# Two blocks on one NeuronCore: both parts of x as 512 moving columns in retention and the first feed-forward

## The chip, the cores and the metric

The kernel runs on one core of a Trainium2 chip. The metric is the device time of one execution in microseconds; below, the median of three runs stands beside the one execution that was taken with the profiler. All times of rows are in microseconds from the start of the profiled span.

## The reference, cut to what matters

Two transformer blocks of depth 2 run one after the other on 256 tokens of width 1024, all in fp32. The first block has a retention mixer, a SwiGLU feed-forward of width 2816, a stick-breaking attention and a mixture of 8 experts; the second block has a hybrid mixer and a convolution feed-forward, twice. The change touches only the first two stages:

```python
def retention_mixer(x, w_in, w_out):
    proj = x @ w_in
    q, k, v, g = split(proj)               # q, k: 4 heads x 256; v, g: 2048 wide
    q, k = rotary(q), rotary(k * 256 ** -0.5)
    ...                                    # scores, state, group norm -> o
    return (silu(g) * o) @ w_out

def swiglu(x, w_in, w_out):
    gate, up = split(x @ w_in, 2)          # 2816 each
    return (silu(gate) * up) @ w_out
```

## The kernel before, in words

**Units.** All weights are cut into units of 128 partitions x 2048 fp32 values (1 MB), which stream through a ring of 13 buffers (`Stream`, from line 33). SyncE's queue loads a raw unit (line 68). ScalarE makes its high part by a copy that rounds to fp32r (`wh`, line 83), VectorE the low part as the difference (`wl`, line 94). `W.advance()`, called behind each unit, splits the next unit for which there is room; at most five split pairs stand at a time (`PAIRS`), so in the steady state each call makes one `wh` and one `wl`, for a unit some five ahead of the one in use, and then issues the next load. The activations x are split in the same way, into `xh` and `xl`, which are two tiles with tags of their own.

**The product of a unit.** `projA` (lines 205 to 217) makes 256 output features for 256 tokens, features on the partitions. For each of two column halves c and each of eight k there are three matmuls of 256 moving columns, all into the same 256 sums: high weights by `xh`, high weights by `xl`, low weights by `xh` (`mm3`, line 200). That is 48 matmuls and 48 weight loads a unit. The result lies in PSUM in a tile with the tag "P"; there are four of these, of one bank each. The other tag, "A", has two tiles of two banks each; the output projections and the transpositions at the end of a stage use it.

**Order.** The order on every engine is that of the program text: the kernel switches the planner off (`manual_schedule`), so that an instruction waits behind all that stand before it on its engine, even if its own inputs are ready. In all three loops `W.advance()` stands at the end of the body, so the two weight splits of a unit stand ahead of the next unit's work on ScalarE and VectorE.

**The three loops.** (1) Query and key, 8 units: `projA`; `rotary` (lines 350 to 358) forms x cos and x sin on VectorE out of PSUM (tiles `t1` and `t2`, tag "wk" with two buffers), and GpSimd makes from both the subtraction and the addition into `qk`. (2) Gate, 8 units: `projA`, silu on ScalarE (line 441), multiplication with the normalised attention `onT` on VectorE (442), high part `yh` on ScalarE (194), low part `yl` on VectorE (195). (3) Feed-forward, 22 units: the first four come with tokens on the partitions and are transposed, the other 18 through `projA`; then silu of the gate half (456), multiplication with the other half (457), `yh`, `yl`.

**Behind loops 2 and 3** stands the output projection (`proj_out`, line 239): it takes two "A" tiles, one for each half of the tokens, and for each weight unit runs 12 matmuls of 512 columns into the first and then 12 into the second.

Of the kernel before, what the change touches and what calls it, by code (L numbers as in the profile page):

```python
# [10 lines left out]
F32 = mybir.dt.float32  # L11
F32R = mybir.dt.float32r
# [3 lines left out]
AF = mybir.ActivationFunctionType  # L16
OP = mybir.AluOpType
PSUM = bass.MemoryType.PSUM

S, D = 256, 1024  # L20
KC = D // 128
# [5 lines left out]
FT = 22  # L27
E = 8
SL = 7
UNIT = 2048  # L30


class Stream:
# [6 lines left out]
    def __init__(self, nc, pool, pairs, count, units):  # L40
        self.nc, self.units = nc, units
        self.pairs = pairs
        self.free = [(pool, "b%d" % i, len(units)) for i in range(count)]
        self.n_load = self.n_h = self.n_l = self.n_get = self.n_done = 0
        self.rt, self.ht, self.held = {}, {}, {}
# [80 lines left out]
def tok(t):  # L126
    return slice(t * 128, t * 128 + 128)
# [6 lines left out]
class Net:  # L134
# [51 lines left out]
        nc.vector.memset(self.eps_rms, RMS_EPS)  # L186

    def new_xT(self):
        xh = self.xT.tile([128, KC, S], F32R, tag="xh", name="xh")
        xl = self.xT.tile([128, KC, S], F32R, tag="xl", name="xl")  # L190
        return xh, xl

    def split(self, h, l, src, eng=None):
        self.nc.scalar.activation(h, src, AF.Copy)  # L194
# [10 lines left out]
    def projA(self, between=None, apart=False):  # L205

        h, l = self.get8()
        ps = [self.psP([128, S]) for _ in range(2)] if apart else self.psP([128, 2, S])
        for c in range(2):
            if c and between:  # L210
                between(ps)
            s = tok(c)
            self.mm3(ps[c] if apart else ps[:, c, :], [p for k in range(KC) for p in (
                (h[:, k, s], self.xh[:, k, :]), (h[:, k, s], self.xl[:, k, :]), (l[:, k, s], self.xh[:, k, :]))])
        self.W.done()
        return ps

    def tokB(self, ps, w, t):
        h, l = w
# [67 lines left out]
            self.W.done()  # L287
            yield ps[i]

    def features(self, first, n, pool):  # L290

        nc, last = self.nc, None

        def copied(ps):
            x = pool.tile([128, 2, 256], F32, tag="fl", name="fl", bufs=2)
            nc.scalar.activation(x, ps, AF.Copy)
            return x

        def flip(x):
            pt = self.psP([128, 2, S])  # L300
            for c in range(2):
                for t in range(2):
                    nc.tensor.transpose(pt[:, c, tok(t)], x[:, t, tok(c)], self.ident)
            return pt

        k = 0
        for ps in first:
            x = copied(ps)
            if last is not None:
                yield flip(last)  # L310
            last = x
            k += 1
        ps = self.projA()
        yield flip(last)
        yield ps
        for _ in range(n - k - 1):
            yield self.projA()

    def rstd(self, var, eps, scale, n=1, tag="rs"):
        sd = self.small(n, tag + "_sd")  # L320
# [5 lines left out]
    def start(self):  # L326
        nc, a = self.nc, self.a
        self.xh, self.xl = self.new_xT()
        W = self.W
        (xr, sx), (t, sw) = W.take(0, "xr", F32), W.take(0, "raw", F32)  # L330
        (h, sh), (l, sl) = W.take(0, "wh"), W.take(0, "wl")
        fh, fl = (x.rearrange("p k s -> p (k s)") for x in (self.xh, self.xl))
        for p in range(4):
            s = half(p)
            nc.sync.dma_start(xr[:, s], a["xT"][:, s])
            nc.sync.dma_start(t[:, s], W.units[0][:, s])
        for p in range(4):
            s = half(p)
            self.split(fh[:, s], fl[:, s], xr[:, s])
            self.split(h[:, s], l[:, s], t[:, s])  # L340
        W.ht[0] = (h, l)
        W.held[0] = [sh, sl]
        W.free += [sx, sw]
        W.n_load = W.n_h = W.n_l = 1
        W.fill()
        W.advance()
        self.x = self.xt.tile([128, 2, D], F32, name="x")
        nc.sync.dma_start(self.x, a["x"])

    def rotary(self, ps, out, cos, sin, scale, pool):  # L350
        nc = self.nc
        t1 = pool.tile([128, 2, S], F32, tag="wk", name="t1", bufs=2)
        t2 = pool.tile([128, 2, S], F32, tag="wk", name="t2", bufs=2)
        for t, cs in ((t1, cos), (t2, sin)):
            nc.vector.scalar_tensor_tensor(t, ps, scale, cs[:, None, :].to_broadcast([128, 2, S]),
                                           op0=OP.mult, op1=OP.mult)
        nc.gpsimd.tensor_tensor(out[:, 0, :], t1[:, 0, :], t2[:, 1, :], op=OP.subtract)
        nc.gpsimd.tensor_tensor(out[:, 1, :], t2[:, 0, :], t1[:, 1, :], op=OP.add)

    def retention(self):  # L360
        nc, tc, a = self.nc, self.tc, self.a
        W = self.W
        with tc.tile_pool(name="r1", bufs=1) as p, tc.tile_pool(name="r2", bufs=2) as w:
# [20 lines left out]
            def pv(h, t):  # L384
                ps = self.psP([128, 512])
                vs = half(h)
                if t == 0:
                    nc.tensor.matmul(ps, lhsT=sc[:, h, :128], rhs=v[:, 0, vs], start=True, stop=True)
                else:
                    nc.tensor.matmul(ps, lhsT=sc[:, h, 128:256], rhs=v[:, 0, vs], start=True, stop=False)  # L390
                    nc.tensor.matmul(ps, lhsT=sc[:, h, 256:], rhs=v[:, 1, vs], start=False, stop=True)
                st = self.sm.tile([128, 6], F32, tag="st1", name="st1")
                nc.vector.bn_stats(st, ps)
                mv = self.small(2, "mv")
                nc.vector.bn_aggr(mv, st)
                r = self.rstd(mv[:, 1:2], self.eps_ln, 1.0)
                on[h, t] = w.tile([128, 512], F32, tag="wk", name="on")
                nc.vector.tensor_scalar(on[h, t], ps, mv[:, 0:1], r, op0=OP.subtract, op1=OP.mult)

            def tr(h, t):  # L400
                o = on.pop((h, t))
                ps = self.psP([128, 4, 128])
                for j in range(4):
                    nc.tensor.transpose(ps[:, j, :], o[:, tok(j)], self.ident)
                nc.scalar.activation(onT[:, 4 * h:4 * h + 4, tok(t)], ps, AF.Copy)

            for i in range(2):
                for h in range(RH):
                    ps = self.projA()
                    self.rotary(ps, qk[:, i, h], cs[:, 0, :], cs[:, 1, :], 1.0, w)  # L410
                    W.advance()
            nc.scalar.preload_act_table_set("sqrt_and_others")
            todo = []
# [17 lines left out]
            yh = p.tile([128, 16, S], F32R, tag="b0", name="yh")  # L431
            yl = p.tile([128, 16, S], F32R, tag="b1", name="yl")
            for j in range(8):
                ps = self.projA(lambda ps: (tr(2, 1), pv(3, 1)) if j == 0 else None)
                if j < 2:
                    tr(3, j)
                if j == 0:
                    nc.scalar.preload_act_table_set("silu_and_others")
                    joint = LayerNorm(self, p, w, 0, "ds")
                sg = w.tile([128, 2, S], F32, tag="wk", name="sg")  # L440
                nc.scalar.activation(sg, ps, AF.Silu)
                nc.vector.tensor_tensor(sg, sg, onT[:, 2 * j:2 * j + 2, :], op=OP.mult)
                self.split(yh[:, 2 * j:2 * j + 2, :], yl[:, 2 * j:2 * j + 2, :], sg)
                W.advance()
# [3 lines left out]
    def ffn(self, joint0):  # L448
        nc, tc, W = self.nc, self.tc, self.W
        with tc.tile_pool(name="f1", bufs=1) as p, tc.tile_pool(name="f2", bufs=2) as w:  # L450
            joint = LayerNorm(self, p, w, 1)
            yh = p.tile([128, FT, S], F32R, name="yh")
            yl = p.tile([128, FT, S], F32R, name="yl")
            for j, ps in enumerate(self.features(self.head(joint0, "silu"), FT, w)):
                sg = w.tile([128, S], F32, tag="sg", name="sg")
                nc.scalar.activation(sg, ps[:, 0, :], AF.Silu)
                nc.vector.tensor_tensor(sg, sg, ps[:, 1, :], op=OP.mult)
                self.split(yh[:, j, :], yl[:, j, :], sg)
                W.advance()
            self.proj_out(yh, yl, FT // 2, joint)  # L460
            return joint
# [140 lines left out]
    def moe(self, joint0):  # L602
        nc, tc, a, W = self.nc, self.tc, self.a, self.W
        with self.span:
# [51 lines left out]
            low_part(0)  # L656
            logits(1)
            high_part(1)
            W.widen([(self.xT, x, self.moe_i + 70) for x in ("xh", "xl")])
            W.pairs = 3  # L660
            W.fill()
            route(1)
# [610 lines left out]
class Joint:  # L1273
# [17 lines left out]
    def trans(self, t):  # L1291
        n, nc = self.n, self.nc
        if t == 0:
            n.xh, n.xl = n.new_xT()
        src = self.src[t]
        for f in range(2):
            q = n.psA()[:, 0, :].rearrange("p (b c) -> p b c", b=4) if t else n.psP([128, 4, 128])
            for j in range(4):
                nc.tensor.transpose(q[:, j, :], src[:, tok(4 * f + j)], n.ident)
            k = slice(4 * f, 4 * f + 4)  # L1300
            n.split(n.xh[:, k, tok(t)], n.xl[:, k, tok(t)], q)
# [258 lines left out]
```

## Time and profile before

| | |
|---|---|
| median of three runs | 2269.43 us (2269.21 to 2270.16) |
| profiled execution | 2271.13 us, span 2269.3 us, mean granted clock 0.992 |
| TensorE busy | 2209.9 us, 97% |
| VectorE busy | 1705.9 us, 75% |
| ScalarE busy | 1374.1 us, 61% |
| GpSimd busy | 63.4 us, 3% |
| DMA | 562.07 MB, mean 248 GB/s |

Busy time is the time with at least one instruction in work. Matmuls are pipelined: the duration shown of one is from its start to its modelled end, while the next one starts much earlier, so the pace is read from start to start. A row `x2` merges two instructions.

### The profile page before, as it was taken

What the parts mean: (1) busy time and instruction counts of PE and PEld (TensorE: products, weight loads), DVE (VectorE), ACT (ScalarE), POOL (GpSimd) and SP (SyncE); (2) the same over time, 40 slices, a digit from 0 to 9 for tenths busy, and PEclk for the clock granted to TensorE, in tenths of its full rate; (3) what the DMA queues carried; (4) which work ended last, traced back from release to release, by engine and by line L of the source; (5) the groups of instructions that cost most, each with busy time, mean ns of one, the idle gap of its engine ahead of it and who ended that gap; (6) DMA issues with size and microseconds to landing.
All of it is one profiled execution on the core that took longest, in us unless ns stands there. A gap on an engine that the chain in (4) does not pass through costs nothing. (4 is left out here: it accounts for less than half of the span.)

```text
span 2269.3 us, 31847 instructions
## 1 busy us (share of the span) xinstructions
PE 2209.9 (97%) x13077; PEld 1922.5 (85%) x13077; DVE 1705.9 (75%) x1671; ACT 1374.1 (61%) x1380; POOL 63.4 (3%) x78
## 2 busy tenths in 40 slices
PE   8999999998999999999999999997999999999998
PEld 8998998987888888878887888886889998888996
DVE  6566554647889888888888888887876975776972
ACT  4353543664777777777776777775556654555752
POOL 4100000010000000000000000000000000000000
PEclk9999999999999999999999999998999999999999
DMA  8444555537988899989998999995234554434551
GB/s 305 163 170 173 200 186 184 174 129 279 397 328 311 303 386 366 352 309 376 355 351 301 345 377 366 353 345 185 94 131 169 205 186 167 151 130 143 204 192 68
DMA packets 80074, 562.07 MB, mean 248 GB/s; under 512 B 9072, under 2 KB 9136, under 8 KB 13488
## 3 DMA queue, kind: packets, MB, share of 16 engines
q1 hardware_dynamic: 76464, 547.39, 65.7%
q0 software_dynamic: 3456, 12.55, 1.7%
q8 instruction: 105, 1.72, 0.3%
q14 instruction: 49, 0.40, 0.0%
HBM read 558.86 MB, written 1.05 MB: 247 GB/s over the span
## 5 line engine op out<-in xcount | busy, mean ns | idle before, releaser
L94 DVE TENSOR_TENSOR wl<-raw,wh 128x2048 fp32r<-128x2048 f32 x518 | 1185.3, 2291 | 318.8 <-ACT wh L83 316.7
L83 ACT ACTIVATE wh<-raw 128x2048 fp32r<-128x2048 f32 x518 | 991.2, 1915 | 393.7 <-PE pp L754 198.7
L200 PE MATMUL pp<-xh,wh 128*128 128x256 f32 x1360 | 389.0, 286 | 7.5 <-ACT wh L194 7.4
L200 PE MATMUL pp<-xh,wl 128*128 128x256 f32 x1360 | 385.6, 283 | 0.1
L200 PE MATMUL pp<-xl,wh 128*128 128x256 f32 x1360 | 384.3, 283 | 0.0
L200 PEld LDWEIGHTS pp<-xh,wh 128*128 128x128 f32 x1360 | 257.0, 189 | 9.3 <-ACT wh L194 8.1
L200 PEld LDWEIGHTS pp<-xl,wh 128*128 128x128 f32 x1360 | 258.8, 190 | 0.5 <-issue 0.5
L200 PEld LDWEIGHTS pp<-xh,wl 128*128 128x128 f32 x1360 | 257.7, 189 | 1.2 <-DVE wl L195 0.9
L200 PE MATMUL pp<-wh,xh 128*128 128x256 f32 x720 | 206.8, 287 | 5.2 <-DVE mix L1139 5.2
L200 PE MATMUL pp<-wh,xl 128*128 128x256 f32 x720 | 203.1, 282 | 0.0
L200 PE MATMUL pp<-wl,xh 128*128 128x256 f32 x720 | 202.6, 281 | 0.0
L754 PE MATMUL pp<-wh,xgh 128*128 128x512 f32 x448 | 179.5, 401 | 3.8 <-DVEq L831 3.8
L754 PE MATMUL pp<-wh,xh 128*128 128x512 f32 x448 | 179.4, 400 | 0.0
L754 PE MATMUL pp<-wl,xgh 128*128 128x512 f32 x448 | 177.2, 396 | 1.5 <-DVE wl L94 1.5
L754 PE MATMUL pp<-wl,xh 128*128 128x512 f32 x448 | 177.7, 397 | 0.7 <-DVE wl L94 0.7
L754 PE MATMUL pp<-wh,xl 128*128 128x512 f32 x448 | 177.6, 396 | 0.0
L754 PE MATMUL pp<-wh,xgl 128*128 128x512 f32 x448 | 177.0, 395 | 0.0
L200 PEld LDWEIGHTS pp<-wh,xh 128*128 128x128 f32 x720 | 136.6, 190 | 7.9 <-issue 6.1
L764 PE MATMUL pa<-wh,hh 128*128 128x512 f32 x448 | 142.0, 398 | 0.7 <-ACT hh L194 0.7
L764 PE MATMUL pa<-wh,hl 128*128 128x512 f32 x448 | 141.4, 397 | 0.0
L764 PE MATMUL pa<-wl,hh 128*128 128x512 f32 x448 | 141.3, 397 | 0.0
L200 PEld LDWEIGHTS pp<-wl,xh 128*128 128x128 f32 x720 | 136.6, 190 | 0.9 <-issue 0.7
(335 smaller groups left out, 3054.4 us busy)
## 6 DMA issues: line engine op xcount, KB each, us to landing
raw<-in_moe_w_in SPq DMA_DIRECT2D x224, 1024.0 KB, 5.4
raw<-in_moe_w_out SPq DMA_DIRECT2D x112, 1024.0 KB, 5.5
raw<-in_w_up SPq DMA_DIRECT2D x44, 1024.0 KB, 4.8
raw<-in_w_in SPq DMA_DIRECT2D x28, 1024.0 KB, 4.8
raw<-in_ret_w_in SPq DMA_DIRECT2D x23, 1024.0 KB, 5.2
raw<-in_ffn_w_in SPq DMA_DIRECT2D x22, 1024.0 KB, 4.8
raw<-in_w_down SPq DMA_DIRECT2D x22, 1024.0 KB, 4.8
raw<-in_ffn_w_out SPq DMA_DIRECT2D x11, 1024.0 KB, 4.8
```

The source lines that it names most:

```text
L83: self.nc.scalar.activation(h, self.rt[i][0], AF.Copy)
L94: self.nc.vector.tensor_tensor(l, r, h.bitcast(F32), op=OP.subtract)
L200: self.nc.tensor.matmul(out, lhsT=w, rhs=x, start=(i == 0), stop=(i == n - 1))
L754: nc.tensor.matmul(q, lhsT=x[:, k, :], rhs=ww[:, kk, :], start=(k == 0 and i == 0), stop=(k == KC - 1 and i == 2))
L764: nc.tensor.matmul(A[0][f], lhsT=x[:, k, :], rhs=ww[:, kk, half(f)], start=(s == 0 and k == 0 and i == 0), stop=(s == SL - 1 and k == 3 an ...
```

## The change

`xh` and `xl` become two halves of one tile (`xx`). A new `projW` takes the place of `projA` in 7 of the 8 query/key units, in the gate units j = 2 to 7 and in the last 17 units of the feed-forward. Per c and k it runs one matmul of 512 moving columns, `xh` and `xl` side by side, over the high weights, and one of 256 columns, `xh` over the low weights, into the first 256 sums: 32 matmuls a unit. Its result lies in an "A" tile, one bank for each c. ScalarE copies the sums of `xl` to SBUF, and VectorE adds those of `xh`; what follows works on this sum in SBUF, in place. In `rotary` the sine product comes first and the cosine product overwrites the sum; both are plain multiplications. In the mixture of experts, the two halves of the x tile that are lent to the ring for a while come out of one tile.

```diff
     def new_xT(self):
-        xh = self.xT.tile([128, KC, S], F32R, tag="xh", name="xh")
-        xl = self.xT.tile([128, KC, S], F32R, tag="xl", name="xl")
-        return xh, xl
+        self.xx = x = self.xT.tile([128, 2, KC, S], F32R, tag="x", name="xx")
+        return x[:, 0], x[:, 1]
...
+    def projW(self, pool, tag):
+        h, l = self.get8()
+        A = self.psA()
+        x = pool.tile([128, 2, S], F32, tag=tag, name="sum", bufs=2)
+        for c in range(2):
+            s, o = tok(c), A[:, c, :].rearrange("p (j s) -> p j s", j=2)
+            for k in range(KC):
+                self.nc.tensor.matmul(o, lhsT=h[:, k, s], rhs=self.xp[:, :, k, :], start=(k == 0),
+                                      stop=(k == KC - 1))
+                self.nc.tensor.matmul(o[:, 0, :], lhsT=l[:, k, s], rhs=self.xh[:, k, :], start=False,
+                                      stop=(k == KC - 1), skip_group_check=True)
+        self.W.done()
+        self.nc.scalar.activation(x, A[:, :, S:], AF.Copy)
+        self.nc.vector.tensor_tensor(x, A[:, :, :S], x, op=OP.add)
+        return x
...
-            yield self.projA()
+            yield self.projW(pool, "fl") if wide else self.projA()
...
-    def rotary(self, ps, out, cos, sin, scale, pool):
+    def rotary(self, ps, out, cos, sin, pool, own):
         nc = self.nc
-        t1 = pool.tile([128, 2, S], F32, tag="wk", name="t1", bufs=2)
+        t1 = pool.tile([128, 2, S], F32, tag="wk", name="t1", bufs=2) if own else ps
         t2 = pool.tile([128, 2, S], F32, tag="wk", name="t2", bufs=2)
-        for t, cs in ((t1, cos), (t2, sin)):
-            nc.vector.scalar_tensor_tensor(t, ps, scale, cs[:, None, :].to_broadcast([128, 2, S]),
-                                           op0=OP.mult, op1=OP.mult)
+        for t, cs in ((t2, sin), (t1, cos)):
+            nc.vector.tensor_tensor(t, ps, cs[:, None, :].to_broadcast([128, 2, S]), op=OP.mult)
...
-                    ps = self.projA()
-                    self.rotary(ps, qk[:, i, h], cs[:, 0, :], cs[:, 1, :], 1.0, w)
+                    first = i == h == 0
+                    ps = self.projA() if first else self.projW(w, "wk")
+                    self.rotary(ps, qk[:, i, h], cs[:, 0, :], cs[:, 1, :], w, first)
                     W.advance()
...
-                sg = w.tile([128, 2, S], F32, tag="wk", name="sg")
+                if j < 2:
+                    sg = w.tile([128, 2, S], F32, tag="wk", name="sg")
+                else:
+                    sg = ps = self.projW(w, "wk")
                 nc.scalar.activation(sg, ps, AF.Silu)
...
-            W.widen([(self.xT, x, self.moe_i + 70) for x in ("xh", "xl")])
+            lent = self.xT.tile([128, 2, UNIT], F32, tag="x", name="lent")
+            W.widen([(Lent(lent[:, i, :]), None, self.moe_i + 70) for i in range(2)])
```

## Rows read from the trace of the kernel before

**Rows 1.** Page, part 1: busy time, share, instructions.
```profile
PE 2209.9 (97%) x13077; PEld 1922.5 (85%) x13077; DVE 1705.9 (75%) x1671; ACT 1374.1 (61%) x1380; POOL 63.4 (3%) x78
```

**Rows 2.** Windows, three stretches: length, busy (instructions) by engine, granted clock, DMA.
```profile
20.00:55.00 35.00, 35.00 (x294) 35.00 (x293) 27.04 (x24) 16.52 (x9) 18.87 (x11) 1.00 0.84 310
...
270.00:300.00 30.00, 30.00 (x252) 30.00 (x251) 18.05 (x17) 13.71 (x17) 0.00 (x0) 1.00 0.58 206
...
1210.00:1211.00 1.00, 1.00 (x4) 0.81 (x3) 1.00 (x1) 0.00 (x0) 0.00 (x0) 0.50 0.08 33
```

**Rows 3.** Timeline of TensorE, output projection: start, duration, instruction.
```profile
170.13 0.63 PE L239 MATMUL pa<-wh,yh 128*128 128x512 f32 x2
...
172.93 0.63 PE L239 MATMUL pa<-wh,yh 128*128 128x512 f32 x2
```

**Rows 4.** Timelines of VectorE and ScalarE, gate units; in brackets idle time and releaser.
```profile
132.12 0.69 DVE L442 TENSOR_TENSOR sg<-sg,onT 128x512 f32<-128x512 f32 x1 [1.75 <-ACT sg L441]
...
137.53 0.68 DVE L442 TENSOR_TENSOR sg<-sg,onT 128x512 f32<-128x512 f32 x1
...
142.93 0.68 DVE L442 TENSOR_TENSOR sg<-sg,onT 128x512 f32<-128x512 f32 x1
...
131.49 0.60 ACT L441 ACTIVATE sg<-pp 128x512 f32<-128x512 f32 x1
...
138.25 0.63 ACT L194 ACTIVATE yh<-sg 128x512 fp32r<-128x512 f32 x1 [1.39 <-DVE sg L442]
...
141.53 0.60 ACT L441 ACTIVATE sg<-pp 128x512 f32<-128x512 f32 x1 [0.84 <-PE pp L200]
```

**Rows 5.** Timelines of VectorE, ScalarE and TensorE, feed-forward and its output projection.
```profile
267.73 0.41 DVE L457 TENSOR_TENSOR sg<-sg,pp 128x256 f32<-128x256 f32 x1
...
272.64 0.42 DVE L457 TENSOR_TENSOR sg<-sg,pp 128x256 f32<-128x256 f32 x1
...
287.87 0.42 DVE L457 TENSOR_TENSOR sg<-sg,pp 128x256 f32<-128x256 f32 x1 [0.40 <-ACT sg L456]
...
257.44 0.37 ACT L456 ACTIVATE sg<-pp 128x256 f32<-128x256 f32 x1
...
287.45 0.38 ACT L456 ACTIVATE sg<-pp 128x256 f32<-128x256 f32 x1 [2.31 <-PE pp L200]
...
347.58 0.63 PE L239 MATMUL pa<-wh,yh 128*128 128x512 f32 x2
```

**Rows 6.** Timelines of VectorE, GpSimd and ScalarE, query/key units.
```profile
37.47 1.29 DVE L355 SCALAR_TENSOR_TENSOR t<-pp,cs 128x512 f32<-128x512 f32 x2 [1.32 <-POOL qk L358]
38.68 2.28 DVE L94 TENSOR_TENSOR wl<-raw,wh 128x2048 fp32r<-128x2048 f32 x1
42.28 1.29 DVE L355 SCALAR_TENSOR_TENSOR t<-pp,cs 128x512 f32<-128x512 f32 x2 [1.32 <-POOL qk L358]
...
29.83 2.80 POOL L358 TENSOR_TENSOR qk<-t,t 128x256 f32<-128x256 f32 x1
...
38.84 2.71 POOL L357 TENSOR_TENSOR qk<-t,t 128x256 f32<-128x256 f32 x1 [1.40 <-DVE t L355]
...
59.59 1.92 ACT L83 ACTIVATE wh<-raw 128x2048 fp32r<-128x2048 f32 x1 [3.84 <-PE pp L200]
```

**Rows 7.** Timelines of ScalarE and VectorE: a copy out of PSUM, and a dependent pair.
```profile
118.22 0.60 ACT L418 ACTIVATE v<-pp 128x512 f32<-128x512 f32 x1 [2.42 <-PE pp L200]
...
217.90 0.68 DVE L1335 SCALAR_TENSOR_TENSOR z<-x,pa 128x512 f32<-128x512 f32 x1
218.62 0.69 DVE L1336 BATCH_NORM_STATS2 st<-z 128x6 f32<-128x512 f32 x1
```

**Rows 8.** Timeline of TensorE in the mixture of experts, behind a long idle time.
```profile
1207.94 0.47 PE L754 MATMUL pp<-wh,xgh 128*128 128x512 f32 x1 [3.84 <-DVEq L831]
...
1208.72 0.57 PE L754 MATMUL pp<-wh,xgh 128*128 128x512 f32 x1
...
1212.08 0.44 PE L754 MATMUL pp<-wh,xgl 128*128 128x512 f32 x1
```

More of the change, by code (lines that the diff above doesn't have):

```diff
@@ L30, with __init__, tile @@
 UNIT = 2048
+class Lent:
+    def __init__(self, ap):
+        self.ap = ap
+    def tile(self, shape, dt, tag, name):
+        return self.ap if dt == F32 else self.ap.bitcast(dt)
 class Stream:
@@ L288, in head, with features @@
             yield ps[i]
-    def features(self, first, n, pool):
+    def features(self, first, n, pool, wide=False):
         nc, last = self.nc, None
@@ L328, in start @@
         self.xh, self.xl = self.new_xT()
+        self.xp = self.xx
         W = self.W
@@ L433, in retention @@
             for j in range(8):
-                ps = self.projA(lambda ps: (tr(2, 1), pv(3, 1)) if j == 0 else None)
                 if j < 2:
+                    ps = self.projA(lambda ps: (tr(2, 1), pv(3, 1)) if j == 0 else None)
                     tr(3, j)
@@ L453, in ffn @@
             yl = p.tile([128, FT, S], F32R, name="yl")
-            for j, ps in enumerate(self.features(self.head(joint0, "silu"), FT, w)):
+            for j, ps in enumerate(self.features(self.head(joint0, "silu"), FT, w, True)):
                 sg = w.tile([128, S], F32, tag="sg", name="sg")
@@ L1294, in trans @@
             n.xh, n.xl = n.new_xT()
+            n.xp = n.xx
         src = self.src[t]
```

## Prediction, written before the changed kernel ran

> **What bounds the kernel now.** I read the busy shares first: TensorE has work 97% of the span, so a microsecond taken from it or put on it counts in full, unless another engine holds it up [rows 1]. Second, the windows give its pace in the stage that is changed: 294 matmuls of 256 columns in 35.0 us, 119 ns each, at granted clock 1.00 [rows 2]. The timeline gives the pace of 512 columns: twelve matmuls from 170.13 to 172.93, 233 ns each [rows 3]. So the price goes almost by columns: two of 256 cost 238 ns, one of 512 costs 233. Third, because the change gives ScalarE and VectorE more to do per unit, I read their timelines in the three loops that it touches. Those engines take instructions in the order written: the multiplication of unit 2 starts at 142.93, the moment the weight split before it lets VectorE go, though its silu was done at 142.13 [rows 4]. What matters is therefore not their busy share, but how long one turn of their dependent chain is against the 5.71 us (48 x 119 ns) of a unit on TensorE.
>
> **Direct part: matmuls.** 30 units change (7 of the query/key units, 6 gate units, 17 of the feed-forward). Each goes from 48 matmuls of 256 columns (48 x 119 = 5.71 us) to 16 of 512 and 16 of 256 (16 x (233 + 119) = 5.63 us): 0.08 us a unit, 2.4 us in all, where TensorE sets the pace. No row shows a 512-column operand made of two pieces of 256; bounds: two separate matmuls, 238 ns, no gain; or the full 2.4 GHz, some 210 ns by the half clock of [rows 2, 8] (420 ns, halved 210), some 0.4 us a unit. I take 233, the nearest row. The Trainium skill, "TensorE: Matmul & The Clock Gate", section "Back-to-back issue gap", has about 131 ns for a sustained matmul of 512 columns; by that a unit would take 16 x (131 + 119) = 4.0 us and 30 units would give back 51 us; the rows have 233, so I keep them. None of this enters the sum below, since in all three loops the end is set by ScalarE and VectorE.
>
> **What is added.** Per unit one ScalarE copy out of PSUM (128x512: 0.60 us) and one VectorE addition that waits for it (0.69, as the multiplication of the same size) [rows 4, 7]. The old product went into one of four PSUM buffers "P"; the new one uses "A", of which there are two. So unit k+2 can't start before the addition of unit k is done; and behind the gate units and the feed-forward the output projection takes the same two buffers, its first token half that of the last unit but one, its second half that of the last unit.
>
> **Gate units.** One turn before: multiplication, high part of y, weight split on ScalarE, weight split on VectorE, next multiplication: 142.93 - 137.53 = 5.40 us, below 5.71, so it catches up [rows 4]. The changed turn starts with the addition: to the silu that needs it 0.72 (as from multiplication to high part, 137.53 to 138.25), silu to multiplication 0.63 (131.49 to 132.12), then the old 5.40: 6.75 us against a unit of 5.63. The lag grows 1.1 us a unit. The first changed unit (j=2) adds at 142.93, where its multiplication starts now; j=7 adds at 142.93 + 5 x 6.75 = 176.68 and ends at 177.37. Two buffers just cover the units themselves (j=5's addition ends at 163.87, when j=7 may start at about 164.1, four units of 5.65 behind the 141.53 at which j=2's product is ready). But the output projection's second half now starts at 172.93 [rows 3], and after the change at 177.42, 0.05 behind the last addition: **+4.5 us**.
>
> **Feed-forward.** One turn now: 272.64 - 267.73 = 4.91 [rows 5]. Added: addition to silu 0.72, silu to multiplication 0.42 (287.45 to 287.87): 6.05 us against 5.63. The first changed unit (j=5) has its copy where its silu stands now, 257.44, since ScalarE is behind there; addition 0.63 later, at 258.07. The 21st adds at 258.07 + 16 x 6.05 = 354.87, ends 355.56. On the way TensorE waits some 0.4 us before each unit; the second half of the output projection starts at 355.61 and not at 347.58 [rows 5]: **+8.0 us**.
>
> **Query/key units.** Here the sum lies in a "wk" buffer, of which there are two, the other holding the sine product; GpSimd reads both, so the next copy waits for GpSimd. One turn: copy 0.60 + 0.03, addition and the gap before an instruction that reads its result 0.72 (217.90 to 218.62, [rows 7]), sine product 0.61, cosine product 0.69, 0.08 to GpSimd, its two subtractions 3.41 (38.84 to 42.25; the first takes 2.71 as VectorE's weight split runs beside it), 0.03: 6.17 us [rows 6]. Now that turn is 42.28 - 37.47 = 4.81, below a unit, and four buffers cover its late start. The first rotary work ends on GpSimd at 32.63 [rows 6]; the second unit's copy then starts at 32.66, its addition ends at 33.98. Unit k+2 starts 0.05 behind addition k: the eighth starts at 33.98 + 4 x 6.17 + 0.05 = 58.71 and ends 5.63 + 0.16 later at 64.5. It ends at 59.57 now, where the ScalarE split that it releases starts (59.59): **+4.9 us**. The split blocked behind the waiting copy is of a unit four ahead, which hides it; the value units behind use "P" and are not held.
>
> **Clock.** The second halves above find TensorE idle 3.95 us (gate units: the first half ends its issue at 173.47) and about 3.2 us (feed-forward). Behind an idle of 3.84 us the granted clock was 0.50, which is 1.2 GHz, and eight matmuls of 512 columns, from 1208.72 to 1212.08, took 3.36 us and not 1.86: 1.5 us lost [rows 2, 8]. I put 1.5 on the gate units and half of it, 0.7, on the feed-forward (bounds 0 and 1.5 each). The first wait in the query/key units, about 3.5 us, is paid inside the GpSimd turn, which is longer than a unit, so a slow unit there is hidden.
>
> **Neighbours at nothing.** One tile for both parts of x, and the lent tile in the mixture of experts, have the same readers and last uses; they cost nothing if each half keeps its own waits; a false wait there would cost about one weight split, 2.28 us [rows 6], at each place. The weights' transfers start later where VectorE frees their buffers later, but they are split four to five units ahead of their use, some 20 us, which covers that.
>
> **Sum.** Profiled execution 2271.13 (span 2269.3, 1.8 around it). 4.9 + 4.5 + 8.0 + 2.2 = 19.6: span 2288.9, execution 2290.7. The three runs' median, 2269.43, is 1.7 under the profiled one; so 2289.0.
>
> **Rivals.**
> (a) *Not slower: the chains don't hold TensorE.* If the addition ran in the free time of VectorE (it is busy 18.05 of 30 us in the feed-forward now [rows 2], 3.4 us a unit, and would be 4.1 of 5.63), the turns stay under a unit and the direct 2.4 us remain: 2267. It decides from a turn of 5.63 us downward. For it: the busy sums. Against: the start at 142.93, behind the split. 8%. By the 131 ns of the Trainium skill's page (section as above) the same rival would end at 2218; against the rows' 233 ns it gets 1 of these 8.
> (b) *Part of the stalls.* The silu and products out of SBUF are quicker than out of PSUM, or GpSimd's start ahead of the split shortens its turn. At 0.4 us less a turn, the feed-forward loses 16 x 0.4 = 6.4 of its 8.0, the gates 2.0 of 4.5, query/key 1.6 of 4.9, and the clock term goes: 2277. 17%.
> (c) *Only the ends count worse*: both idle times lower the clock in full, and false waits on the joint tile add a split at two places: 2295. 7%.
> (d) *The change doesn't do what it says*: two-piece operands run as two: no different here, 2289, as the chains set the end; it has its chance in the forecast's.
>
> **How the numbers follow.** Forecast 67%, with 2283 to 2294 its own range (0.2 us a turn on 16 + 5 + 4 turns is 5 us; the clock 2). Range: down to (b) with a little less, up to (c): 2273 to 2295. A measurement of this kernel tells 0.2% (4.5 us) from no change. Faster: 4% (half of (a), if the 512 columns are near the lower bound of 210 ns). Same: 9% (the other half of (a), and 5 of (b) at its lowest). Slower: 87%, the rest.
>
> **What would show it.** Right: additions 6.0 to 6.1 us apart in the feed-forward and 6.7 apart in the gates; TensorE's idle time before the "pa" matmuls put down to the addition, with some 4 and 3 us at the output projections; query/key units over 6 us apart. Wrong: matmuls of the changed units without gaps and the output projection starting with the last unit; or 512-column matmuls well under 230 ns with the stage shorter than now.

## The result and the profile after

| | before | after |
|---|---|---|
| median of five runs | 2269.28 us (2269.20 to 2270.16) | 2292.37 us (2291.55 to 2293.51) |
| profiled execution, span | 2271.13, 2269.3 us | 2291.55, 2289.5 us |
| TensorE busy, matmuls | 2209.9 us, 13077 | 2213.1 us, 12597 |
| VectorE, ScalarE busy | 1705.9, 1374.1 us | 1725.8, 1389.9 us |

After over before is 1.0099 (95% interval 1.0087 to 1.0110): 23 us slower, against a forecast of 2289.0. There are 480 matmuls fewer (30 x 16), and ScalarE and VectorE have 30 instructions more each, as meant. The time lies in waits. These are the waits of TensorE's weight loads from 20 to 400 us in the changed kernel (us in total, times, longest):

```profile
PEld pa L235 <- DVE sum L241: 14.1, 19, 3.6
PEld pa L265 <- DVE sum L241: 9.4, 4, 4.1
```

L235 is the wide matmul of a unit, L265 the output projection, L241 the new addition. The two rows are not the loss itself: by the same list for matmuls, TensorE stood idle for 16.0 us before them.

```profile
PE pa L235 <- DVE sum L241: 8.1, 19, 3.3
PE pa L265 <- DVE sum L241: 7.9, 4, 3.7
```

The next rows are TensorE's matmuls that waited, in the same kernel: the first wait of the query/key units, the two halves of the retention's output projection, one of the repeated waits of the feed-forward, and the second half of its output projection.

```profile
33.52 0.80 PE L235 MATMUL pa<-xx,wh 128*128 128x512 f32 x1 [3.29 <-DVE sum L241]
...
175.63 0.74 PE L265 MATMUL pa<-wh,yh 128*128 128x512 f32 x2 [0.91 <-DVE sum L241]
182.41 0.74 PE L265 MATMUL pa<-wh,yh 128*128 128x512 f32 x2 [3.70 <-DVE sum L241]
...
306.56 0.50 PE L235 MATMUL pa<-xx,wh 128*128 128x512 f32 x1 [0.22 <-DVE sum L241]
...
367.48 1.18 PE L265 MATMUL pa<-wh,yh 128*128 128x512 f32 x2 [3.02 <-DVE sum L241]
```

The second halves began at 172.93 [rows 3] and 347.58 [rows 5] before. VectorE in the same kernel shows the turns: gate units first, then feed-forward.

```profile
147.74 0.68 DVE L241 TENSOR_TENSOR sum<-pa,sum 128x512 f32<-128x512 f32 x1
...
154.53 0.68 DVE L241 TENSOR_TENSOR sum<-pa,sum 128x512 f32<-128x512 f32 x1
...
181.67 0.68 DVE L241 TENSOR_TENSOR sum<-pa,sum 128x512 f32<-128x512 f32 x1
...
269.26 0.69 DVE L241 TENSOR_TENSOR sum<-pa,sum 128x512 f32<-128x512 f32 x1
...
275.36 0.68 DVE L241 TENSOR_TENSOR sum<-pa,sum 128x512 f32<-128x512 f32 x1
...
366.74 0.68 DVE L241 TENSOR_TENSOR sum<-pa,sum 128x512 f32<-128x512 f32 x1
```

From 147.74 to 181.67 are five turns, 6.79 us each; from 269.26 to 366.74 sixteen, 6.09 us each. Each addition starts without idle time, and all but the one at 269.26 right behind a weight split, though the ScalarE copy was done before. For the one at 154.53 the copy and the split are:

```profile
152.19 0.57 ACT L240 ACTIVATE sum<-pa 128x512 f32<-128x512 f32 x1
...
152.32 2.29 DVE L104 TENSOR_TENSOR wl<-raw,wh 128x2048 fp32r<-128x2048 f32 x1 [1.11 <-ACT wh L93]
```

In the query/key units the copy waits for GpSimd (ScalarE, 6.30 us from copy to copy):

```profile
38.43 0.60 ACT L240 ACTIVATE sum<-pa 128x512 f32<-128x512 f32 x1 [3.89 <-POOL qk L384]
...
44.73 0.60 ACT L240 ACTIVATE sum<-pa 128x512 f32<-128x512 f32 x1 [3.90 <-POOL qk L384]
```

Three kinds of marks cut the difference into terms: the first multiplication of the gate units (132.12 [rows 4], then 136.93), the second halves above, and the last norm statistics behind each stage (VectorE, before and then after, with the first gate multiplication after):

```profile
220.66 0.21 DVE L1315 BATCH_NORM_AGGREGATE mv<-st 128x2 f32<-128x12 f32 x1
...
412.12 0.21 DVE L1315 BATCH_NORM_AGGREGATE mv<-st 128x2 f32<-128x12 f32 x1
```

```profile
136.93 0.69 DVE L472 TENSOR_TENSOR sg<-sg,onT 128x512 f32<-128x512 f32 x1 [1.76 <-ACT sg L471]
...
231.79 0.21 DVE L1347 BATCH_NORM_AGGREGATE mv<-st 128x2 f32<-128x12 f32 x1
...
433.67 0.21 DVE L1347 BATCH_NORM_AGGREGATE mv<-st 128x2 f32<-128x12 f32 x1
```

| term | forecast | measured | from the marks |
|---|---|---|---|
| query/key | +4.9 | +4.8 | 136.93 - 132.12 |
| gates | +4.5 | +4.7 | (182.41 - 172.93) - 4.8 |
| clock behind the gates | +1.5 | +1.65 | (231.79 - 220.66) - 9.48 |
| feed-forward | +8.0 | +8.8 | (367.48 - 347.58) - 11.13 |
| clock behind the feed-forward | +0.7 | +1.65 | (433.67 - 412.12) - 19.90 |
| sum | +19.6 | +21.55 | |

The spans differ by 20.2. The last 1.35 us come back far from the change, in the last hybrid mixer: there the kernel before lost clock behind a wait of 2.58 us, and the profiled execution after did not behind one of 2.64 us. Windows of that place, before and then after (granted clock before the last two columns):

```profile
2030.00:2050.00 20.00, 17.42 (x116) 15.47 (x115) 14.49 (x37) 9.47 (x21) 0.00 (x0) 0.91 0.48 175
```

```profile
2050.00:2070.00 20.00, 17.36 (x130) 15.46 (x129) 14.64 (x41) 10.66 (x25) 0.00 (x0) 1.00 0.52 187
```

The profiled execution is the fastest of the five; the others are up to 2 us longer. The profiled execution before was 1.9 us over its median. So the two traces differ by 20.4 us of time, and the medians by 23.1.

### The profile page after: what moved, and what is told of

Its sections match the earlier page's. It is cut to its first block, busy times and chain, and to the rows that moved or that the text cites. A ratio compares the mean times of both kernels' runs of the same rounds, so it can differ in the third digit from the quotient of the medians.

```text
span 2289.5 us, 30933 instructions
## 1 busy us (share of the span) xinstructions
PE 2213.1 (97%) x12597; PEld 1896.5 (83%) x12597; DVE 1725.8 (75%) x1701; ACT 1389.9 (61%) x1410; POOL 63.5 (3%) x78
## 3 DMA queue, kind: packets, MB, share of 16 engines
q8 instruction: 101, 1.65, 0.3%
## 5 line engine op out<-in xcount | busy, mean ns | idle before, releaser
L209 PE MATMUL pp<-xx,wh 128*128 128x256 f32 x1760 | 323.3, 285 | 7.8 <-ACT wh L203 7.8
L785 PE MATMUL pp<-wh,xx 128*128 128x512 f32 x896 | 293.4, 398 | 0.0
L209 PEld LDWEIGHTS pp<-xx,wh 128*128 128x128 f32 x1760 | 273.6, 190 | 9.8 <-ACT wh L203 8.1
L209 PE MATMUL pp<-wh,xx 128*128 128x256 f32 x1440 | 267.0, 284 | 5.3 <-DVE mix L1170 5.2
L209 PE MATMUL pp<-xx,wl 128*128 128x256 f32 x880 | 249.8, 284 | 0.1
L209 PEld LDWEIGHTS pp<-wh,xx 128*128 128x128 f32 x1440 | 224.0, 189 | 8.6 <-issue 6.2
L209 PE MATMUL pp<-wl,xx 128*128 128x256 f32 x720 | 202.0, 281 | 0.0
L785 PEld LDWEIGHTS pp<-wh,xx 128*128 128x128 f32 x896 | 168.7, 188 | 40.0
L235 PE MATMUL pa<-xx,wh 128*128 128x512 f32 x480 | 172.7, 400 | 8.1 <-DVE sum L241 8.1
L785 PE MATMUL pp<-wl,xx 128*128 128x512 f32 x448 | 177.7, 397 | 0.7 <-DVE wl L104 0.7
L209 PEld LDWEIGHTS pp<-xx,wl 128*128 128x128 f32 x880 | 167.0, 190 | 0.8 <-DVE wl L204 0.8
L265 PE MATMUL pa<-wh,yh 128*128 128x512 f32 x360 | 115.7, 403 | 7.9 <-DVE sum L241 7.9
```

Of the source, the lines that this page charges most:

```text
L209: self.nc.tensor.matmul(out, lhsT=w, rhs=x, start=(i == 0), stop=(i == n - 1))
L235: self.nc.tensor.matmul(o, lhsT=h[:, k, s], rhs=self.xp[:, :, k, :], start=(k == 0), stop=(k == KC - 1))
L265: self.nc.tensor.matmul(acc[:, f, :], lhsT=x[:, k, s], rhs=ww[:, kk, half(f)], start=(first and kk == 0 and i == 0), stop=(last and kk == ...
L785: nc.tensor.matmul(q, lhsT=x[:, k, :], rhs=ww[:, kk, :], start=(k == 0 and i == 0), stop=(k == KC - 1 and i == 2))
```

## The experiments

Theory: each changed unit makes the dependent chain through ScalarE, VectorE (and GpSimd) longer than a unit on TensorE, and two PSUM buffers let that reach TensorE. Rivals: the amount of added work, the wide two-piece operand, the joint tile, or the two buffers by themselves. Ratios below are against the kernel before on the same chip, whose median was 2270.54 us in the first four and 2269.76 in the last four.

**Only the joint tile (`joint`).** All of `projW` undone, `xx` and `lent` kept.

```diff
-                    ps = self.projA() if first else self.projW(w, "wk")
+                    ps = self.projA()
...
-                    sg = ps = self.projW(w, "wk")
+                sg = w.tile([128, 2, S], F32, tag="wk", name="sg")
...
-            for j, ps in enumerate(self.features(self.head(joint0, "silu"), FT, w, True)):
+            for j, ps in enumerate(self.features(self.head(joint0, "silu"), FT, w)):
```

> Of the change only the joint tile for both parts of x and the lent tile remain; all units run as before. Theory (dependent chains on ScalarE, VectorE and GpSimd against two PSUM buffers): the tile costs nothing, 2269.3 us within 0.5. Rival (a false wait on the joint tile carries part of the 23 us): some 2.3 us for each such wait, 2271.6 or more.

Measured: 2270.60 us, ratio 1.0002 (0.9993 to 1.0011). In its trace the first gate multiplication and both last norm statistics stand 0.28 us earlier than in the kernel before (131.84, 220.38 and 411.84). The joint tile costs nothing that can be measured.

**The wide matmul cut into two (`two256`).**

```diff
-                self.nc.tensor.matmul(o, lhsT=h[:, k, s], rhs=self.xp[:, :, k, :], start=(k == 0),
-                                      stop=(k == KC - 1))
+                for j, xx in enumerate((self.xh, self.xl)):
+                    self.nc.tensor.matmul(o[:, j, :], lhsT=h[:, k, s], rhs=xx[:, k, :], start=(k == 0 and j == 0),
+                                          stop=(k == KC - 1), skip_group_check=True)
```

> The changed kernel, but the 512 columns over the high weights run as two matmuls of 256 columns: 48 matmuls and weight loads a unit again, all else as changed. Theory: the chains set the end, so the 0.08 us a unit of TensorE is hidden behind turns of 6.1 to 6.8 us: as the changed kernel, 2292.4 within 1.5. Rival (TensorE's pace with the wide operand made of two pieces, or the count of weight loads, decides): a few us away, 2289 if the two-piece operand costs, 2295 if it saves.

Measured: 2293.73 us (2292.28 to 2295.28), ratio 1.0102 (1.0087 to 1.0118), beside 1.0099 for the changed kernel. Its second halves start at 182.64 and 367.71, both 0.23 us later than in the changed kernel, and its first gate multiplication does too: the 23 units of gates and feed-forward, in another matmul form, moved nothing in between. So in these two stages the difference in TensorE's pace does not set the time. In the query/key units it is otherwise: the first addition is 0.37 us earlier than in the changed kernel (32.40 against 32.77), TensorE waits for it until 33.14, then runs at half clock to about 39.3, and has no further wait in this loop. There its own pace, with the clock, set the end. Its profile is 1.2 us longer behind 367.71 for another reason, told in the last section.

**No copy and no addition (`nosum`).** The sums of the low part of x over the high weights are left out. The two rotary products go to tiles of their own again.

```diff
-        x = pool.tile([128, 2, S], F32, tag=tag, name="sum", bufs=2)
...
-        self.nc.scalar.activation(x, A[:, :, S:], AF.Copy)
-        self.nc.vector.tensor_tensor(x, A[:, :, :S], x, op=OP.add)
-        return x
+        return A[:, :, :S]
...
-                    self.rotary(ps, qk[:, i, h], cs[:, 0, :], cs[:, 1, :], w, first)
+                    self.rotary(ps, qk[:, i, h], cs[:, 0, :], cs[:, 1, :], w, True)
...
```

> The changed kernel without the copy and the addition: what follows reads the sums of the high part of x straight out of PSUM tile A (the sums of the low part over the high weights are left out of the result). 32 matmuls a unit and two buffers A remain. Theory: turns are back at 4.8 to 5.4 us, under a unit of 5.6, so the gates and the feed-forward lose nothing; only the first buffer wait in the query/key units stays, about 3.5 us, and the slower clock behind it, 1.2; the direct 2.4 us come back: 2272 (2269 to 2274). Rival (two buffers alone cost it): 2280 or more.

Measured: 2271.39 us, ratio 1.0004 (0.9995 to 1.0014). Two buffers and 32 matmuls a unit stay, and the time is back to that of the kernel before. One long wait remains, as was expected. TensorE, and the windows behind it:

```profile
34.19 0.77 PE L234 MATMUL pa<-xx,wh 128*128 128x512 f32 x1 [3.38 <-DVE t L379]
```

```profile
34.00:36.00 2.00, 1.81 (x5) 1.59 (x6) 2.00 (x2) 1.79 (x1) 1.88 (x1) 0.50 0.97 274
36.00:38.00 2.00, 2.00 (x8) 1.67 (x7) 0.69 (x2) 0.00 (x0) 1.52 (x2) 0.50 0.97 381
38.00:40.00 2.00, 2.00 (x8) 1.71 (x7) 2.00 (x3) 0.00 (x0) 1.08 (x1) 0.50 1.01 418
```

In the gates and the feed-forward two buffers alone cost next to nothing: one wait of 0.4 us. In the query/key units they cost as much as the whole change: the first gate multiplication stands at 137.44, 5.3 us later than before and later than in the changed kernel (136.93). The wait of 3.4 us and half the clock up to about 40.0 (nine pairs of matmuls take 5.9 us, not 3.2) make that up. Behind the gates `nosum` is 4.4 us late, behind the feed-forward 2.1 (last norm statistics at 225.03 and 414.17): with nothing to wait for, its quicker units save in these two stages 3.3 of the 5.3 us that the first one lost.

**Four units deep (`deep`).** Copy and addition kept; pairs of units alternate between A and pairs of P banks, so that the output projections find A free.

```diff
+        if inP:
+            A = [self.psP([128, 512]) for _ in range(2)]
+        else:
+            t = self.psA()
+            A = [t[:, c, :] for c in range(2)]
...
-            yield self.projW(pool, "fl") if wide else self.projA()
+            yield self.projW(pool, "fl", (n - 1 - j) // 2 % 2 == 0) if wide else self.projA()
...
+                    sg = ps = self.projW(w, "wk", (7 - j) // 2 % 2 == 0)
...
```

> The changed kernel with copy and addition, but pairs of units alternate between the two A tiles and pairs of P banks (two copies and two additions of 256 columns each where P is used): four units deep, and the output projections find A free. Turns stay longer than a unit; the lag grows to some 13 us in the feed-forward and is covered by four buffers. Theory: no wait of TensorE, 2267.0 (2266 to 2269.5). Rival (the added work itself costs, 60 instructions of some 20 us on each of two engines, whatever the buffers): 2285 or more.

Measured: 2266.80 us, ratio 0.9983 (0.9974 to 0.9992), faster than both kernels. The turns are as long as in the changed kernel (VectorE, 6.10 us):

```profile
333.26 0.68 DVE L251 TENSOR_TENSOR sum<-pa,sum 128x512 f32<-128x512 f32 x1
...
339.36 0.68 DVE L251 TENSOR_TENSOR sum<-pa,sum 128x512 f32<-128x512 f32 x1
```

but TensorE no longer waits for an addition: its weight loads' list for 20 to 400 us, which the changed kernel begins with 14.1 and 9.4 us, now begins

```profile
PEld pp L427 <- issue: 1.9, 8, 0.2
PEld pp L209 <- issue: 1.9, 8, 0.2
```

and the output projection, which starts at 340.09, runs while the last additions are still to come (at 345.46 and 351.28). The query/key turns are still 6.30 us (additions at 39.69 and 45.99), and yet the first gate multiplication stands at 131.08, 5.85 us earlier than in the changed kernel. All the added work is still done, so its amount is not what costs.

**One stage at a time (`only_qk`, `only_gate`, `only_ffn`).** `projW` in one loop only.

> Of the changed units only the seven of query and key; gates and feed-forward as before. Theory: the GpSimd turn alone, as the trace of the changed kernel has it, +4.8 us: 2274.1 (2273 to 2275.5). Rival (the stages lean on each other, a lag carried from one into the next): under +3 or over +7.

> Of the changed units only the six gate units. Theory: +4.7 us for the wait at the output projection and +1.7 for the lower clock behind it: 2275.7 (2274 to 2277). Rival (the wait is only moved from the query/key units): no more than +3.

> Of the changed units only the seventeen of the feed-forward. Theory: +8.7 us of longer turns and the end, +1.7 for the lower clock: 2279.7 (2278 to 2281.5). Rival (it is the clock or a lag brought along that costs there, not the turn of 6.09 us): under +6.

Measured: query/key 2275.94 us, ratio 1.0025 (1.0015 to 1.0035); gates 2277.26, 1.0031 (1.0019 to 1.0043); feed-forward 2281.07, 1.0049 (1.0034 to 1.0064). Less 2269.76 these are 6.2, 7.5 and 11.3 us, 25.0 together; the change had 23.1. Each is 1.4 to 1.8 us over the time expected, the first two just beyond the bounds given; 0.5 us of this is that the kernel before was slower here than the 2269.3 that the expectations start from. In the query/key kernel 0.7 of it is seen. Its weights arrived later (the ScalarE split that waits for a load at 22.96 in the changed kernel does so at 23.67 here), its first addition starts at 33.52 and not at 32.77, and the chain carries this on: the first gate multiplication stands at 137.59, against 136.93 in the changed kernel and 131.84 with the joint tile alone. The rest is within what the runs of each kernel scatter (1.7 to 2.8 us). The waits stay where the whole change has them (gates: 3.72 us at 177.66; feed-forward: 3.03 at 356.03), so the stages don't lean on each other.

**The weight splits moved (`early`).** Gates and feed-forward changed, query/key as before; the same instructions and buffers in another order. The gate loop is edited in the same way, from j = 2.

```diff
+                if j > 4:
+                    W.advance()
                 nc.scalar.activation(sg, ps[:, 0, :], AF.Silu)
                 nc.vector.tensor_tensor(sg, sg, ps[:, 1, :], op=OP.mult)
                 self.split(yh[:, j, :], yl[:, j, :], sg)
-                W.advance()
+                if j <= 4:
+                    W.advance()
```

> Gate units and feed-forward changed, query and key as before; the two weight splits of a unit are moved from behind its work to between the addition and the silu. Same instructions, same two buffers, another order. One turn of the feed-forward is then copy 0.50, split on ScalarE 1.93, split on VectorE 2.21, multiplication 0.45, high part 0.35: 5.44 us, under a unit of 5.63; of the gates 5.9, over it by 0.27. Theory (the order of the chain decides): waits of under 1 us in all, 2268.3 (2267 to 2271). Rival (the amount of added work decides): as the sum of the two stages, 2286.

Measured: 2268.13 us, ratio 0.9991 (0.9982 to 1.0000). The turn of the feed-forward is 5.40 us (VectorE, additions):

```profile
301.04 0.69 DVE L241 TENSOR_TENSOR sum<-pa,sum 128x512 f32<-128x512 f32 x1
...
306.44 0.69 DVE L241 TENSOR_TENSOR sum<-pa,sum 128x512 f32<-128x512 f32 x1
```

that of the gates 5.88 (additions at 154.23 and 160.11), and TensorE waits twice for an addition:

```profile
PEld pa L235 <- DVE sum L241: 0.9, 1, 0.9
...
PEld pa L265 <- DVE sum L241: 0.6, 1, 0.6
```

These are 1.5 us together, where under 1 was expected; the time came out as expected. The two stages that lost 18.8 us on their own lose nothing when the splits stand elsewhere in the chain. That is the closest test of the theory for these two stages: amount of work, buffers and matmuls are all the same. It says nothing of query/key.

## Why the prediction was right, and where its sizes were off

The mechanism held: the chains are longer than a unit, the lag grows, and it is paid where the output projection asks for the buffer of the last unit, and all along in the query/key loop and the feed-forward. In the gates and the feed-forward a shorter chain (`early`), more buffers (`deep`) or leaving out the added pair (`nosum`) each removes the loss; TensorE's form of matmul (`two256`) and the joint tile (`joint`) do not matter. In the query/key units only more buffers (`deep`) removed it. In the changed kernel's trace the turn sets the end there, but one wait for two buffers and the lower clock behind it cost as much without it (`nosum`); what the long turn alone would cost is not shown.

The terms are 1.95 us short together (19.6 against 21.55), the forecast of the median 3.4. Most of the rest is scatter: the forecast took 1.7 us off because the profiled execution before was slower than its median, while the profiled execution after was 0.8 us faster than its own. The chances given to the cases add up to 99%.

**What is added; gates.** Forecast 6.75 us a turn, measured 6.79, the silu out of SBUF taking 0.63 us (148.46 to 149.09) where the one out of PSUM took 0.60; +4.5 became +4.7. The two buffers did not quite cover the last unit: it waited 0.29 us (168.84), which costs nothing, since its own addition comes later still. The clock behind it, 1.5, was 1.65.

**Feed-forward.** 6.05 us a turn were forecast and 6.09 measured, over sixteen turns 0.7 us: the silu out of SBUF takes 0.42 us where the one out of PSUM took 0.38 [rows 5]. So +8.0 became +8.8. Rival (b), that reading SBUF is quicker, had the sign wrong for the silu.

**Query/key.** The turn was 6.30 and not 6.17. The cosine product, which overwrites the sum in place, starts 0.73 behind the sine product (34.22 behind 33.49), not the 0.61 of two products into different tiles; with the first addition ending earlier (33.46, forecast 33.98) the stage still came to +4.8. That is luck: the two errors, of 0.5 us each, cancel, and the eighth unit starts at 58.72, forecast 58.71.

```profile
58.72 0.50 PE L235 MATMUL pa<-xx,wh 128*128 128x512 f32 x1 [0.44 <-DVE sum L241]
```

The slow clock behind the first wait was to be hidden in the turn. In the changed kernel it was: it lasted to about 36.5. In `two256` and `nosum` it lasted to about 39.3 and 40.0 and was not hidden.

**Clock.** The half put on the feed-forward's wait was too little: a wait of 3.02 us brought the clock down as one of 3.70 did. Windows behind the gates' and the feed-forward's wait in the changed kernel:

```profile
184.00:186.00 2.00, 2.00 (x6) 1.56 (x5) 0.69 (x1) 2.00 (x2) 0.00 (x0) 0.50 0.93 393
...
369.00:371.00 2.00, 2.00 (x7) 1.54 (x5) 0.62 (x2) 1.58 (x1) 0.00 (x0) 0.51 0.95 401
```

**Direct part.** This term was mis-sized, though it was rightly kept out of the sum. I took 119 ns a matmul from a count over a window, which also counts instructions that reach over its edges [rows 2]. From start to start, two units of the kernel before stand 5.76 us apart, 120 ns a matmul: the silu at 287.45 [rows 5] and the one before it,

```profile
281.69 0.39 ACT L456 ACTIVATE sg<-pp 128x256 f32<-128x256 f32 x1 [1.47 <-PE pp L200]
```

and twelve pairs of the changed unit take 4.21 us, 351 ns a pair:

```profile
36.70 0.40 PE L235 MATMUL pa<-xx,wh 128*128 128x512 f32 x1
36.94 0.28 PE L237 MATMUL pa<-xx,wl 128*128 128x256 f32 x1
37.06 0.39 PE L235 MATMUL pa<-xx,wh 128*128 128x512 f32 x1
...
40.91 0.39 PE L235 MATMUL pa<-xx,wh 128*128 128x512 f32 x1
```

That is 5.61 us a unit, 0.15 saved and not 0.08: 4.5 us for 30 units. `deep`, where nothing waits, measures 3.7 us (1.8 to 5.9). Of the pair's 351 ns the narrow matmul takes 0.12 us (36.94 to 37.06), as before. That leaves some 0.23 us for 512 columns in two pieces, the same as in one [rows 3]. The 131 ns of the Trainium skill, "TensorE: Matmul & The Clock Gate", section "Back-to-back issue gap", are not seen here in either form.

## What to carry to other kernels

On engines that take their instructions in order, a loop's limit is one turn of its dependent chain over all engines, in written order, and not any engine's busy share: add up that turn from start to start before adding an instruction to it. A chain longer than the bottleneck engine's unit is free as long as buffers cover the lag (`deep`), and is paid at the place that asks for the last buffer; a deeper rotation or moving independent work to another place in the chain (here the weight splits) gives the gain back. The saving itself must be measured from unit to unit, not by a count over a window.

## What the runs showed of the hardware that I had not expected

- The stretch at the lower clock (1.2 GHz) differs behind nearly equal waits. Behind 3.02 us at the same place it ended at about 371.0 in the changed kernel and at about 373.8 in `two256` (3.5 and 6.1 us after TensorE began again), which is the 1.2 us by which the latter is longer there: 0.50 still in its window

```profile
371.00:373.00 2.00, 2.00 (x7) 1.54 (x6) 2.00 (x1) 0.00 (x0) 0.00 (x0) 0.50 0.11 45
```

- Behind a wait of about 2.6 us the clock may be lower or not: 0.91 and 1.00 in the two windows of the last hybrid mixer above, in code that the change doesn't touch. It moved 1.4 to 1.6 us there between two executions. Of the eight traces here with this wait (2.57 to 2.64 us), three show 0.50 behind it (the kernel before, `nosum`, `only_gate`) and five 1.00 throughout. Why is open.
